# A tenth gate and up pair by seven products in place of two whole hidden tiles, in a two-layer encoder

## The chip, the cores and the metric

The kernel runs on one core of one Trainium2 chip. Its time is the device time of one launch in microseconds (us); the median over the runs is compared. Engines are named as in the profile: PE (TensorE, with PEld for its weight loads), DVE (VectorE), ACT (ScalarE), POOL (GpSimd) and SP (SyncE, which here issues DMAs).

## The reference, cut to what matters

Two encoder layers over 512 tokens of width 1024, in float32. Each has an attention part and a feed-forward part (SwiGLU), each part with a root-mean-square norm in front of it and one behind it:

```
for layer in range(2):
    h = rms_norm(x, attn_pre_g[layer])
    y = mla_mixer(h, ...) if layer == 0 else chunked_mixer(h, ...)
    x = x + rms_norm(y, attn_post_g[layer])
    h = rms_norm(x, ffn_pre_g[layer])
    f = (silu(h @ w_gate) * (h @ w_up)) @ w_down      # 1024 -> 2816 -> 1024
    x = x + rms_norm(f, ffn_post_g[layer])
```

The change concerns `h @ w_gate` and `h @ w_up` of both layers and the steps just ahead of them.

## The kernel before, in words

Activations are kept transposed: features on the 128 partitions, 512 tokens along the row. x is eight tiles of 128 x 512. A matrix product is done in three passes on numbers split into a high and a low part (`split`, lines 143 to 149: ScalarE makes the high part, VectorE the low part as the difference); `mm3` (line 376) is the three matmuls high x high, high x low and low x high. So each weight chunk that is loaded (a `raw` tile, 128 x 1024, of which there are five) costs a cast on ScalarE, `whi`, and a subtraction on VectorE, `wlo`, before TensorE can use it. There are three buffers of split weights.

`Feed` (line 264) holds the plan of all weight chunks in the order of their use. `feed.next` hands out the next chunk and first calls for the split of the chunks behind it, one or two ahead; `feed.ahead` calls for more of them early. `feed.behind[n]` names instructions that the split of chunk n has to be queued behind on their engines; `behind` and `tc.issue_after` do the same for other instructions. Otherwise each engine's order of work follows the order in which the program writes its instructions: the earlier written goes first, but one that isn't ready lets later ones pass, as planned when the program is built. `first(n)` puts an instruction n places forward. On the chip each engine works its list in that order.

**The feed-forward part, `ffn` (line 1134).** The attention's output projection (`out_proj`, line 687) runs its last two groups in two halves of 256 tokens each. Behind each half the post norm's squares are summed (`Post.half`, `Post.add_half`, line 634), and `Post.apply` (line 667) adds the normed result to x half by half and splits x into `xs` (lines 672, 674, 148 and 149). x itself is fetched from memory at the start of `ffn` (`fetch`, line 679).

The hidden width 2816 is 22 tiles of 128, and each needs a gate and an up product over K = 1024. Before the change:

- Tiles f = 0 and 1 (weights `w_gu0`) are made in two halves of 256 tokens, `half(0)` and `half(1)`, as x becomes ready.
- Tiles f = 2 and 3 (weights `w_gu`) are made whole, 512 tokens a matmul, by `proj` (line 382): 96 matmuls.
- The other 18 tiles are nine pairs (`products`, line 1520). A pair takes its two gate and two up tiles by the seven products of Strassen's scheme instead of eight: rows of K and tokens are halved, sums of weight blocks are multiplied with sums of x blocks. Each product j = 0 to 6 is 24 matmuls of 256 columns, 168 in a pair. The x-sums `tb` are made once a layer by `blocks_of` (line 1315) in three steps, `next(more)` each: the first gives what product 0 uses, the second product 3, the third products 4 and 5; products 1, 2 and 6 use x itself. The weight sums are made by accumulating DMAs on the GpSimd queue (`Pair.begin`, line 164, called for the next pair during this one) and by VectorE (`Pair.sums`, line 182); for the first pair, VectorE makes all of them.

The results of a pair are gathered in `gate` and `up_` tiles as its products end (lines 1553 to 1566). After product 6 come the gates: times the norm's factor `rb` (line 1567), silu on ScalarE (1568), times up (1570), and `Hidden.add` (line 1257), which makes four sums of 256 columns out of two tiles. The norm of the feed-forward's input is applied there, on the outputs. Its squares (`sx.squares`, line 760) are summed over the partitions by four transposes (`tot`, line 473), raised to the power -1/2 on GpSimd (483) and spread by four transposes (`bc`, 501) while the whole tiles run.

In the second layer `by_tokens` (line 1215) also transposes the kept x on VectorE during the pairs. `down` (line 1286) multiplies by `w_down`, again by seven products.

PSUM has eight banks: four called `mm`, two `s` and two `t`. Hidden tiles and x-sums' intermediates lie in a pool `h` of 40 tiles, x, its splits and the splits of the x-sums in a pool `u` of 39.

Of the kernel before, what the change touches and what calls it, by code (L numbers as in the profile page):

```python
# [14 lines left out]
OP = mybir.AluOpType  # L15
# [12 lines left out]
N_WHOLE = 4  # L28
# [40 lines left out]
def trunk(ctx: ExitStack, tc: tile.TileContext, a, out):  # L69
# [80 lines left out]

    class Pair:
# [4 lines left out]
        def __init__(self, src):  # L156
            self.src, self.raw, self.then, self.made = src, {}, None, False

        def tile(self, n, pool_=wp, tag="raw", bufs=5):
            t = pool_.tile([P, 1024], F32, tag=tag, name=name_("raw"), bufs=bufs)  # L160
            nc.sync.dma_start(t, self.src[n])
            return t

        def begin(self):

            r, self.made = self.raw, True
# [6 lines left out]
        def load(self, j):  # L173

            if j == 0:
                if not self.made:
                    self.raw[4] = self.tile(2, wide[0], "sum2", 2)
                self.raw[5] = self.tile(3)
            elif j in (1, 2):
                self.raw[j] = self.tile(j - 1)  # L180

        def sums(self, j):
# [4 lines left out]
            if j == 0 and not self.made:  # L187
                r[0] = r[3] = r[6] = wide[0].tile([P, 1024], F32, tag="sum", name=name_("raw"), bufs=2)
                plus(r[0], r[4], r[5])
            elif j in (3, 6):  # L190
                plus(r[j], r[j], r[j // 3])
            elif j == 4 and not self.made:
                plus(r[4], r[4], r[1])
            elif j == 1 and self.then:
                self.then.begin()
# [68 lines left out]
    class Feed:  # L264


        def __init__(self):
            self.plan, self.raw, self.ready, self.pos, self.room = [], [], [], 0, {}
            self.behind, self.gate, self.low = {}, None, None
# [4 lines left out]
        def add_pairs(self, src):  # L274
# [14 lines left out]
        def load(self, i):  # L289
            while len(self.raw) <= min(i, len(self.plan) - 1):  # L290
# [5 lines left out]
                if isinstance(src, Pair):  # L296
                    src.load(j)
# [314 lines left out]
    class Post:  # L612
# [21 lines left out]
        def add_half(self, h, banks, rest, n1, n2, end=None):  # L634
# [32 lines left out]
        def apply(self, x, h, each, to=None):  # L667
            c = HALF[h]
            for k in range(KT):
                t = self.y[k][:, c]  # L670
                with first(80 * h):
# [5 lines left out]
                    each(k, h)  # L677

    def fetch(src, make=U):
        x = []  # L680
        for k in range(KT):
            t = make(name="x")
            nc.sync.dma_start(t, src[:, k])
            x.append(t)
        return x

    def out_proj(rhs, n_k, post, have, n_last, late):
# [35 lines left out]
        for h in range(2):  # L723
# [17 lines left out]
            if not h:  # L741
                feed.ahead(3)
# [40 lines left out]
    def plan_ffn(i):  # L783
        for c in range(4):
            feed.add(a["w_gu0"][i, c], 1024, room="h")
        for f in range(N_WHOLE - 2):
            for c in range(2):
                feed.add(a["w_gu"][i, f, c], 1024)
# [345 lines left out]
    def ffn(i, x_src, osp, firsts, late=()):  # L1134
# [38 lines left out]
        tb = []  # L1173
        more = blocks_of(x, G_FPRE[i], H, tb)
        next(more)
        b = [bank(), bank()]
        rest = proj(2, KT, 4, xs, b)
        some(rest, 3)
        v = sx.sum.total()
        r = rstd(v)  # L1180
        eps = sp.tile([P, 4], F32, tag="eps", name=f"eps_{i}", bufs=1)
        V.tensor_scalar(eps, v, EPS, None, op0=OP.mult)
        some(rest, 7)
        rb = spread_sb(r)
        next(more)
        banks.extend(b)
        hid = Hidden(H)


        for f in range(N_WHOLE):  # L1190
            if f < 3:
                b = banks[2 * f:2 * f + 2]
                if f == 2:
                    run(rest)
            else:
                b = [bank(), bank()]
                run(proj(2, KT, 4, xs, b))
            t = U(name="gt")
            V.tensor_tensor(t, b[0], rb, op=OP.mult)
            nc.scalar.activation(t, t, AF.Silu)  # L1200
            h = hid.room()
            V.scalar_tensor_tensor(h, t, -1.0, b[1], op0=OP.mult, op1=OP.mult)
            hid.add(h)
            if f == 1:
                next(more)
        products(xs, tb, rb, hid, by_tokens(H) if i else None)
# [108 lines left out]
    def blocks_of(x, gain, make, out):  # L1315
# [3 lines left out]
        for k in range(KT // 2):  # L1319
            out.append([(U(F32R, "th"), U(F32R, "tl")) for _ in range(2)])  # L1320
# [9 lines left out]
        for k in K2:  # L1330
# [3 lines left out]
            split(*cut(out[k][0], A1), m[:, A1])  # L1334
        yield
        for k in K2:
# [3 lines left out]
            split(*out[k][1], n)  # L1340
        yield

    class After:
# [3 lines left out]
        def __init__(self, layer, eps, make):  # L1347
# [4 lines left out]
            self.x, self.later = None, []  # L1352
# [74 lines left out]
        def during(self, j, i):  # L1427
            if j == Down.E3 and i == 1:
                self.x = fetch(a["mid"])
# [90 lines left out]
    def products(xs, tb, rb, hid, aside=None):  # L1520
# [5 lines left out]
                  [cut(xs[k + K2], A1) for k in range(K2)]]  # L1526
        pairs = (NF - N_WHOLE) // 2
        for p in range(pairs):
            al, ga = [], []
            be = [bank("t" if p % 2 else "s", "be") for _ in range(2)]  # L1530
            gate = [U(name="gt") for _ in range(2)]
            up_ = [U(name="ut") for _ in range(2)]
            for j in range(7):
# [10 lines left out]
                for e in range(2):  # L1544
# [10 lines left out]
                    elif j == 1:  # L1555
                        nc.scalar.copy(t[:, A0], o)
                    elif j == 2:
                        V.tensor_tensor(t[:, A0], t[:, A0], o, op=OP.add)
# [6 lines left out]
                    else:  # L1565
                        V.tensor_tensor(t[:, A1], t[:, A1], o, op=OP.add)
                        V.tensor_tensor(t, t, rb, op=OP.mult)
                        nc.scalar.activation(t, t, AF.Silu)
                        h = hid.room()
                        V.tensor_tensor(h, t, u, op=OP.mult)  # L1570
                        hid.add(h)
# [286 lines left out]
```

## Time and profile before

| | us |
|---|---|
| median of 3 runs | 1105.76 (1105.74 to 1106.14) |
| profiled execution | 1109.37 |
| its span, first to last instruction | 1107.4 |

The columns of the page's engine table are busy time, share of the span and count. Rows of the timeline give the start, the length, engine, line, operation, result<-inputs and shape, and in brackets the idle time before it with what ended it; a length includes an end that overlaps the next instruction, so that the distance between starts is the price in a full queue. Rows of the waits give the time waited in all, how often and the longest.

### The profile page before, as it was taken

Reading aid. Unit: us, or ns where it says so; the run is one execution under the profiler, and the core shown is the slowest. Engines: PE = TensorE matmul, PEld = TensorE weight load, DVE = VectorE, ACT = ScalarE, POOL = GpSimd, SP = SyncE. Lnnn points to the kernel's source line nnn. Section 1 sums busy time; section 2 is a strip of 40 time slices with the busy share of each in tenths; the row PEclk is TensorE's granted clock in tenths of the full one; section 3 lists DMA queues with packets and bytes.
Section 4 is the critical chain, followed back from the end, with each engine's and each line's share of the span. In section 5 each row is a group of like instructions: output and inputs, shape, how many; then the busy total and the mean of one; then the engine's idle time right before and its main releaser. Section 6 shows DMA issues by size and latency. Waiting matters only on the chain. (4 is left out here: it accounts for less than half of the span.)

```text
span 1107.4 us, 19059 instructions
## 1 busy us (share of the span) xinstructions
PE 1094.4 (99%) x6893; PEld 979.9 (88%) x6893; DVE 909.3 (82%) x1659; ACT 680.5 (61%) x1323; POOL 117.1 (11%) x181
## 2 busy tenths in 40 slices
PE   9999999999999999999999999999999999999997
PEld 6887889999999998888888888889999999998885
DVE  6787747988878879978857898758988889789977
ACT  7476638555555556668636677657645555556675
POOL 1211100100000001500000110000100010001401
PEclk9999999999999999999999999999999999999999
DMA  7444216538778657961556677634638878858913
GB/s 238 114 122 125 79 59 227 161 103 194 173 196 202 161 184 236 162 192 49 190 152 154 179 192 186 160 128 162 186 106 214 227 197 212 233 176 247 173 29 76
DMA packets 88335, 181.47 MB, mean 164 GB/s; under 512 B 26817, under 2 KB 28609, under 8 KB 88241
## 3 DMA queue, kind: packets, MB, share of 16 engines
q1 hardware_dynamic: 74752, 147.10, 43.5%
q0 software_dynamic: 13056, 32.73, 16.8%
q8 instruction: 54, 0.88, 0.3%
q10 hardware_dynamic: 432, 0.44, 0.1%
q14 instruction: 41, 0.33, 0.1%
HBM read 148.88 MB, written 10.88 MB: 144 GB/s over the span
## 5 line engine op out<-in xcount | busy, mean ns | idle before, releaser
L144 ACT CAST whi<-raw 128x1024 fp32r<-128x1024 f32 (+3 forms) x220 | 221.7, 1008 | 208.7 <-PE al L1550 69.4
L145 DVE TENSOR_TENSOR wlo<-raw,whi 128x1024 fp32r<-128x1024 f32 (+3 forms) x220 | 256.5, 1167 | 69.4 <-ACT whi L144 68.3
L1550 PE MATMUL al<-th,whi 128*128 128x256 f32 x432 | 122.9, 284 | 0.2 <-ACT gt L1560 0.2
L1550 PE MATMUL al<-tl,whi 128*128 128x256 f32 x432 | 121.1, 280 | 0.0
L1550 PE MATMUL al<-th,wlo 128*128 128x256 f32 x432 | 121.1, 280 | 0.0
L377 PE MATMUL b<-xh,whi 128*128 128x512 f32 x234 | 96.7, 414 | 0.0
L379 PE MATMUL b<-xh,wlo 128*128 128x512 f32 x234 | 91.9, 393 | 0.2 <-DVE wlo L145 0.2
L378 PE MATMUL b<-xl,whi 128*128 128x512 f32 x234 | 91.7, 392 | 0.0
L1550 PEld LDWEIGHTS al<-th,whi 128*128 128x128 f32 x432 | 81.4, 188 | 2.5 <-ACT gt L1560 0.4
L1550 PEld LDWEIGHTS al<-tl,whi 128*128 128x128 f32 x432 | 81.4, 189 | 0.0
L1550 PEld LDWEIGHTS al<-th,wlo 128*128 128x128 f32 x432 | 81.4, 188 | 0.0
L548 ACT ACTIVATE p<-p,mn 128x128 f32<-128x128 f32 (+1 forms) x96 | 54.3, 565 | 35.2 <-DVE mn L546 33.3
L145 DVE TENSOR_TENSOR ptl<-pt,pth 128x128 fp32r<-128x128 f32 (+1 forms) x96 | 46.7, 487 | 31.1 <-ACT pth L144 30.2
L145 DVE TENSOR_TENSOR wlo<-wd,whi 128x512 fp32r<-128x512 f32 x86 | 56.5, 689 | 14.6 <-ACT whi L144 14.4
L144 ACT CAST whi<-wd 128x512 fp32r<-128x512 f32 x86 | 49.9, 619 | 25.0 <-PE al L1306 10.7
L144 ACT CAST pth<-pt 128x128 fp32r<-128x128 f32 (+1 forms) x96 | 40.5, 424 | 32.1 <-PE pt L561 31.2
L171 POOL DMA_DIRECT2D raw<-in_w_pair x32 | 28.1, 897 | 287.9 <-DMA raw<-in_w_pair 94.6
L379 PEld LDWEIGHTS b<-xh,wlo 128*128 128x128 f32 x234 | 43.9, 188 | 10.5 <-DVE wlo L145 0.9
L1306 PE MATMUL al<-whi,pl 128*128 128x512 f32 x132 | 51.5, 390 | 0.0
L1306 PE MATMUL al<-whi,ph 128*128 128x512 f32 x132 | 51.4, 390 | 0.0
L1306 PE MATMUL al<-wlo,ph 128*128 128x512 f32 x132 | 51.3, 389 | 0.0
L184 DVE TENSOR_TENSOR raw<-raw,raw 128x1024 f32<-128x1024 f32 x40 | 48.9, 1223 | 0.5
(320 smaller groups left out, 3393.7 us busy)
## 6 DMA issues: line engine op xcount, KB each, us to landing
raw<-in_w_pair SPq DMA_DIRECT2D x88, 512.0 KB, 4.6
raw<-in_w_pair POOLq DMA_DIRECT2D x32, 512.0 KB, 7.5
wd<-in_w_down SPq DMA_DIRECT2D x54, 256.0 KB, 5.7
raw<-in_w_o SPq DMA_DIRECT2D x16, 512.0 KB, 3.8
raw<-in_w_gu SPq DMA_DIRECT2D x16, 512.0 KB, 4.8
raw<-in_w_down SPq DMA_DIRECT2D x16, 512.0 KB, 4.4
raw<-in_w_qkb SPq DMA_DIRECT2D x16, 512.0 KB, 3.6
wd<-in_w_down POOLq DMA_DIRECT2D x22, 256.0 KB, 5.4
```

What stands on the lines that cost most here:

```text
L144: return (nc.scalar.copy(dst_hi, src), V.tensor_tensor(dst_lo, src, dst_hi.bitcast(F32), op=OP.subtract))
L145: V.tensor_tensor(dst_lo, src, dst_hi.bitcast(F32), op=OP.subtract))
L171: nc.gpsimd.dma_start(r[j], self.src[n], accum_op=OP.add)
L184: V.tensor_tensor(t, x, y, op=OP.add)
L377: nc.tensor.matmul(o, l[0], r[0], start=start, stop=False)
L378: nc.tensor.matmul(o, l[0], r[1], start=False, stop=False)
L379: last_mm[0] = nc.tensor.matmul(o, l[1], r[0], start=False, stop=stop)
L548: nc.scalar.activation(p[:, :n], p[:, :n], AF.Exp, bias=mn[:, :1], scale=-1.0, accum_out=self.sums[:, qt:qt + 1])
L1306: nc.tensor.matmul(to[e], l[c], r[d], start=j < 4 and k == 0 and n == 0, stop=k == NF // 2 - 1 and n == 2, skip_group_check=True)
L1550: nc.tensor.matmul(o, l[c], r[d], start=first_ and n == 0, stop=k == K2 - 1 and n == 2, skip_group_check=True)
```

## The change

The two whole tiles go and a tenth pair takes their place: only tiles 0 and 1 stay as they are (`N_WHOLE` is 2). The first pair follows `half(1)` directly. Its weight sums are begun like the others' by DMAs, and it takes its products in the order 1, 2, 0, 3, 6, 4, 5. The first two steps of `blocks_of` are written ahead of the first pair, the third at its product 0. The four banks of tiles 0 and 1 are copied to `kept` tiles by ScalarE.

The squares of x are taken in the second pair, the norm's sum and spread in the third, and with them the gates of tiles 0 and 1. The gates of pairs one to three are held back: they are written at (2,6), (3,1) and (3,4), where (p, j) is product j of pair p counted from 0. From the fourth pair on the gates come at the end of the pair as before. x is fetched behind the loads of the first pair's first weights, and the splits of the next six weights are queued behind the post norm's last squares as well as behind its factor.

```diff
-N_WHOLE = 4
+N_WHOLE = 2
...
+    FIRST_TURN = (1, 2, 0, 3, 6, 4, 5)
...
+            if not h:
+                with behind(feed.loaded):
+                    next(p for p, *_ in feed.plan[feed.pos:] if isinstance(p, Pair)).begin()
             for n in range(len(feed.ready), len(feed.ready) + 6):
-                feed.behind[n] = fence
+                feed.behind[n] = fence + ins
...
             if not h:
-                feed.ahead(3)
+                feed.ahead(3 if late else 5)
+                feed.loaded = get_x(feed.loads[feed.pos + 5])
...
-        x = fetch(x_src)
+        x = []
         post = Post(G_APOST[i], H)
-        last = out_proj(osp, KT, post, firsts, 2, late)
+        last = out_proj(osp, KT, post, firsts, 2, late, lambda after: fetch(x_src, x, after))
...
-        sx.squares(0)
-        post.apply(x, 1, sx.each)
+        feed.behind[next(n for n in range(feed.pos, feed.pos + 9) if feed.plan[n][2] == 0)] = post.apply(x, 1, sx.each)
+        tb, hid = [], Hidden(H)
+        more = blocks_of(x, G_FPRE[i], H, tb)
+        next(more)
         run(half(1))
-        sx.squares(1)
...
+        kept = [H(name="fu") for _ in banks]
+        for t, b in zip(kept[:2], banks[:2]):
+            nc.scalar.copy(t, b)
+        turned = next(more)
+        feed.behind[feed.pos + 3] = turned
+        with behind(turned[0]):
+            for t, b in zip(kept[2:], banks[2:]):
+                empty = nc.scalar.copy(t, b)
...
+        def gates():
+            for f in range(N_WHOLE):
+                t, u = kept[2 * f:2 * f + 2]
+                V.tensor_tensor(t, t, rb[0], op=OP.mult)
+                nc.scalar.activation(t, t, AF.Silu)
+                h = hid.room()
+                V.scalar_tensor_tensor(h, t, -1.0, u, op0=OP.mult, op1=OP.mult)
+                hid.add(h)
...
+        def step():
+            feed.behind[feed.pos + 3] = next(more)
+
+        side = {(0, 0): step, (1, 1): lambda: sx.squares(0), (1, 4): lambda: sx.squares(1), (2, 1): norm,
+                (2, 3): spread_, (2, 4): gates, (2, 6): lambda: held[0](), (3, 1): lambda: held[1](),
+                (3, 4): lambda: held[2]()}
+        products(xs, tb, rb, hid, side, held, (empty, turned[1]), by_tokens(H) if i else None)
...
-            for j in range(7):
+            for j in (range(7) if p else FIRST_TURN):
+                if (p, j) in side:
+                    side[p, j]()
                 if aside is not None and p and j in (0, 1, 3, 5):
                     next(aside, None)
                 w = feed.next(1024, 2)
...
+                        if p > 2:
+                            gated(t, u)
+
+            if p < 3:
+                held.append(lambda gate=gate, up_=up_: [gated(t, u) for t, u in zip(gate, up_)])
```

`norm` is the sum of the squares and the power, `spread_` the four transposes `bc` with their copy, `gated` the gate steps of a pair as before. The rest of the diff lays out the weights for ten pairs, hands the new arguments through, and takes the held gate and up tiles of the first three pairs from pool `h`.

More of the change, by code (lines that the diff above doesn't have):

```diff
@@ L149, in split_scaled @@
                 V.scalar_tensor_tensor(dst_lo, src, col, dst_hi.bitcast(F32), op0=OP.mult, op1=OP.subtract))
+    FIRST_TURN = (1, 2, 0, 3, 6, 4, 5)
     class Pair:
         def __init__(self, src):
-            self.src, self.raw, self.then, self.made = src, {}, None, False
+            self.src, self.raw, self.then, self.turn = src, {}, None, range(7)
         def tile(self, n, pool_=wp, tag="raw", bufs=5):
             t = pool_.tile([P, 1024], F32, tag=tag, name=name_("raw"), bufs=bufs)
-            nc.sync.dma_start(t, self.src[n])
+            self.last = nc.sync.dma_start(t, self.src[n])
             return t
         def begin(self):
-            r, self.made = self.raw, True
+            r = self.raw
             r[0] = r[3] = r[6] = self.tile(2, wide[0], "sum", 2)
@@ L186, in sums @@
             r = self.raw
[L187 to L190, printed above, removed]
+            if j in (3, 6):
                 plus(r[j], r[j], r[j // 3])
-            elif j == 4 and not self.made:
-                plus(r[4], r[4], r[1])
-            elif j == 1 and self.then:
+            if j == (3 if self.turn[0] else 1) and self.then:
                 self.then.begin()
@@ L268, in __init__ @@
             self.plan, self.raw, self.ready, self.pos, self.room = [], [], [], 0, {}
-            self.behind, self.gate, self.low = {}, None, None
+            self.behind, self.gate, self.low, self.loads = {}, None, None, {}
         def add(self, src, n, gain=None, room=None):
@@ L279, in add_pairs @@
                 pair.then = pairs[p + 1] if p + 1 < n else None
-                for j in range(7):
+                if not p:
+                    pair.turn = FIRST_TURN
+                for j in pair.turn:
                     self.plan.append((pair, 1024, j, None))
@@ L296, in load @@
                 if isinstance(src, Pair):
-                    src.load(j)
+                    self.loads[len(self.raw)] = src.load(j)
                     self.raw.append(None)
@@ L676, in apply, with fetch, out_proj @@
                         (nc.gpsimd if k in (0, 2, 4) else V).tensor_tensor(to(k), x[k][:, c], t, op=self.op)
[L677 to L687, printed above, removed]
+                    at = each(k, h)
+            return at
+    def fetch(src, x, after=None):
+        with behind(after):
+            for k in range(KT):
+                t = U(name="x")
+                ins = nc.sync.dma_start(t, src[:, k])
+                x.append(t)
+        return ins
+    def out_proj(rhs, n_k, post, have, n_last, late, get_x):
         done = list(have)
@@ L1176, in ffn @@
[L1176 to L1180, printed above, removed]
-        eps = sp.tile([P, 4], F32, tag="eps", name=f"eps_{i}", bufs=1)
[L1182 to L1205, printed above, removed]
@@ L1206, in ffn, with norm @@
-        products(xs, tb, rb, hid, by_tokens(H) if i else None)
+        kept = [H(name="fu") for _ in banks]
[6 more added lines that the diff above has]
+                empty = nc.scalar.copy(t, b)
+        eps = sp.tile([P, 4], F32, tag="eps", name=f"eps_{i}", bufs=1)
+        rb = []
+        def norm():
+            v = sx.sum.total(None, 300)
+            with first(300):
+                r = rstd(v)
+            V.tensor_scalar(eps, v, EPS, None, op0=OP.mult)
+            rb.append(r)
@@ L1319, in blocks_of @@
         for k in range(KT // 2):
-            out.append([(U(F32R, "th"), U(F32R, "tl")) for _ in range(2)])
+            out.append([tuple(m(F32R, n) for n in ("th", "tl")) for m in (U, make if k == 3 else U)])
         K2 = range(KT // 2)
@@ L1518, in plus_x, with products @@
                 queue.dma_start(rows_of(i)[:, o * S:o * S + S][:, c], t[:, c])
-    def products(xs, tb, rb, hid, aside=None):
+    def products(xs, tb, rb, hid, side, held, turned, aside=None):
         K2 = KT // 2
```

48 lines of the change are left out of this document (23 added, 25 removed).

## The prediction

> **What bounds the kernel now.** I read the page first: its engine table, then who waited for whom on TensorE, then the busy time of the engines in the stretches that the change replaces.
>
> ```profile
> span 1107.4 us, 19059 instructions
> PE 1094.4 (99%) x6893; PEld 979.9 (88%) x6893; DVE 909.3 (82%) x1659; ACT 680.5 (61%) x1323; POOL 117.1 (11%) x181
> ```
>
> ```profile
> PE bc L501 <- POOL r L483: 0.9, 2, 0.7
> PE b L377 <- ACT y L621: 0.8, 1, 0.8
> PE al L1550 <- ACT gt L1560: 0.2, 1, 0.2
> ```
>
> ```profile
> core 0: us, PE busy (x) PEld busy (x) DVE busy (x) ACT busy (x) POOL busy (x), PEclk, DMA share, GB/s
> 213.64:236.39 22.75, 22.75 (x106) 18.81 (x105) 20.36 (x42) 13.70 (x23) 2.91 (x3) 1.00 0.33 70
> 236.39:256.30 19.91, 19.91 (x169) 19.77 (x168) 17.16 (x25) 10.98 (x17) 0.87 (x1) 1.00 0.58 154
> 256.30:276.20 19.90, 19.90 (x170) 19.77 (x169) 16.68 (x24) 10.95 (x17) 2.16 (x3) 1.00 0.76 185
> 790.60:813.32 22.72, 22.72 (x107) 18.80 (x105) 20.63 (x44) 13.84 (x23) 3.22 (x3) 1.00 0.33 71
> 813.32:833.03 19.71, 19.71 (x169) 19.71 (x168) 16.89 (x24) 10.98 (x17) 0.84 (x1) 1.00 0.54 154
> ```
>
> TensorE is busy for 99% of the span, and the waits of its instructions in the feed-forward layers are the three rows above, under 2 us together. So it is the bound there: whatever takes matmul time away shortens the run, as long as nothing new makes TensorE wait. The third view shows where such a wait could come from. Its first and fourth rows are the two whole hidden tiles that the change replaces (f = 2 and 3 of layers 1 and 2); the rows behind them are pairs. VectorE is busy for 20.4 of 22.8 us in the whole tiles and 16.7 of 19.9 in a settled pair. It has 2 to 3 us to spare in each, and no more.
>
> **TensorE's work.** Two whole tiles are 96 matmuls of 512 columns, a pair is 168 of 256. The whole tiles' stretch also holds eight small transposes, for the norm's sum and its spread, which the change keeps and moves into the third pair:
>
> ```profile
> 215.72 0.60 PE L473 MATMUL tot<-ident,acc 128*128 128x128 f32 x4
> 216.07 0.48 PE L377 MATMUL b<-xh,whi 128*128 128x512 f32 x1
> 220.96 0.60 PE L501 MATMUL bc<-ident,r 128*128 128x128 f32 x4
> 221.32 0.48 PE L377 MATMUL b<-xh,whi 128*128 128x512 f32 x1
> ```
>
> From start to start they take 0.35 + 0.36 = 0.71 us. So a layer gives up 22.75 - 0.71 = 22.04 us and gets 19.90 for the tenth pair: 2.1 us less, and 4.2 us less in both layers (22.72 in the second). An eighth of the arithmetic would be 2.8 us in a layer; the rest goes because a column costs more in narrow matmuls, 22.04 / 96 = 0.230 us for 512 against 19.90 / 168 = 0.118 for 256. [...] The trace has durations for both, and I stay with 4.2.
>
> **VectorE's queue in the first pair.** The 22 us that go were also cover: behind them VectorE made the x-sums (`blocks_of`) and the squares, before a pair needed anything. Now the first pair starts when the first two tiles end (213.64 in this trace), and its product j = 6, the fifth in its turn, is due 4 x 2.84 = 11.4 us later, at 225.0. Durations from start to start:
>
> ```profile
> 199.81 0.75 DVE L672 TENSOR_TENSOR y<-y,bc 128x256 f32<-128x256 f32 x2
> 200.47 0.76 DVE L674 TENSOR_TENSOR x<-x,y 128x256 f32<-128x256 f32 x2
> ...
> 201.47 0.89 DVE L149 SCALAR_TENSOR_TENSOR xl<-x,gains,xh 128x256 fp32r<-128x256 f32 x2
> 202.28 0.42 DVE L674 TENSOR_TENSOR x<-x,y 128x256 f32<-128x256 f32 x1
> ```
>
> ```profile
> 276.76 0.42 DVE L1566 TENSOR_TENSOR gt<-gt,be 128x256 f32<-128x256 f32 x1
> 277.21 0.69 DVE L1567 TENSOR_TENSOR gt<-gt,bc 128x512 f32<-128x512 f32 x1
> 277.82 1.22 DVE L145 TENSOR_TENSOR wlo<-raw,whi 128x1024 fp32r<-128x1024 f32 x1
> 278.96 1.29 DVE L1570 TENSOR_TENSOR hd<-gt,ut 128x512 f32<-128x512 f32 x2
> 280.16 0.42 DVE L1271 TENSOR_TENSOR hs<-hd 128x256 f32<-128x256 f32 x1
> 280.50 0.42 DVE L1273 TENSOR_TENSOR hs<-hd,hd 128x256 f32<-128x256 f32 x1
> 280.83 0.42 DVE L1272 SCALAR_TENSOR_TENSOR hs<-hs,hd 128x256 f32<-128x256 f32 x1
> 281.17 1.22 DVE L145 TENSOR_TENSOR wlo<-raw,whi 128x1024 fp32r<-128x1024 f32 x1
> 282.30 0.42 DVE L1274 SCALAR_TENSOR_TENSOR hs<-hs,hd 128x256 f32<-128x256 f32 x1
> 282.64 1.22 DVE L184 TENSOR_TENSOR raw<-raw,raw 128x1024 f32<-128x1024 f32 x1
> 283.77 1.22 DVE L145 TENSOR_TENSOR wlo<-raw,whi 128x1024 fp32r<-128x1024 f32 x1
> ```
>
> So 256 columns take 0.34 us, an `xl` 0.40, 512 columns 0.60, a weight's low half (`wlo`) or weight sum 1.14. VectorE can begin the second half of `apply` at 199.81, as now. What the program puts ahead of product 6's weights is then: `apply`, 8 x (0.34 + 0.34 + 0.40) = 8.6; the x-sums of the first two steps, 16 x 0.34 = 5.4, and of the third, 8 x 0.34 + 4 x 0.60 = 5.1; the weights of j = 0 and 3, one of them a sum first, 3 x 1.14 = 3.4; the two additions of j = 2, 0.7; and its own sum and low half, 2.3. That is 25.5 us from 199.81, so 225.3: 0.3 us late if VectorE never pauses. The third step is written ahead of product 6's weights though only j = 4, behind it, needs it. Bounds: nothing if the order slips in favour of product 6, 2.5 if the ScalarE cast between the sum and the low half (1 us) is not covered and the weights of j = 4 go first (1.1). I take 1.2 us in each layer, the middle. That `begin` now leaves the first pair's two weight sums to DMAs costs VectorE nothing and saves it 2.3, counted above. The four bank copies and the first two steps' casts lie on ScalarE, busy for 13.7 of 22.75 us here: nothing.
>
> **VectorE's queue in the third and fourth pairs.** A pair's own list is seven low halves (8.0), two sums (2.3) and six additions (2.0), 12.2 us. Its gates are 2 x 0.61 + 2 x 0.60 + 4 x 0.34 = 3.8 more, together 16 of 19.9. The change holds the gates of the whole tiles and of pairs one to three until the norm's spread, ahead of product j = 3 in the third pair, and issues them at (2,4), (2,6), (3,1) and (3,4). Pairs three and four have 2 x (19.9 - 12.2) = 15.4 us for them, of which the first four sevenths of pair three, 4.4 us, have gone by; four lots of 3.8 us are 15.0. In the queue: three lots stand ahead of the weights of product j = 3 of pair four. From about 1 us before (2,4) to the start of (3,3) are 6 x 2.84 + 1 = 18.0 us; in it belong 11.3 of gates, the low halves of j = 6 and of four more products and one sum, 6.8, and four additions, 1.3: 19.4, so 1.4 late. VectorE can't run far ahead, since a weight's cast waits until TensorE has done with the buffer, three products back:
>
> ```profile
> ACT whi L144 <- PE al L1550: 69.4, 63, 1.7
> ```
>
> That lead is used up in this count. Bounds: nothing, if the lead is a product larger, and 3.4 if the sum of j = 6 and one low half more are still to be made. I take 1.6 in each layer. In the second layer transposes of the kept x fall into the same stretch:
>
> ```profile
> L1222 DVE STREAM_TRANSPOSE xt<-x x8: 703/709/715, 841.8 to 942.9; 128x512 f32<-128x512 f32 x8
> ```
>
> One or two of 0.7 us: 0.6 more there, between 0 and 1.4. Squares fall into pair two, where no gates stand now: 16 x 0.34 = 5.4 against 7.7 free, nothing.
>
> **x fetched later, splits behind the post norm.** The eight x tiles are now issued behind the loads of the first pair's weights:
>
> ```profile
> L683 SPq DMA_DIRECT2D x<-in_x x8: 328/439/710, 164.0 to 168.6; - x8
> ...
> DMA to landing us min/median/max: 5.8/6.3/7.4
> ```
>
> ```profile
> 169.90 9.63 SPq L303 DMA_DIRECT2D raw<-in_w_gu x6
> ```
>
> ```profile
> 185.64 0.42 DVE L674 TENSOR_TENSOR x<-x,y 128x256 f32<-128x256 f32 x1
> ```
>
> The six weight loads behind x now go out until 179.5; four of them will go ahead of it. So by my estimate x is issued from about 176 to 181 and lands, 6.3 us later, from 182 to 187. The first tile is wanted at 185.64 and each next about 1.1 us later. I take nothing; 2 us a layer if the weight buffers free up late. On the other side, weight casts are now put behind the post norm's squares, and this is a wait of layer 2 that can go:
>
> ```profile
> 757.49 1.05 ACT L144 CAST whi<-raw 128x1024 fp32r<-128x1024 f32 x1 [0.46 <-DMA raw<-in_w_gu]
> 758.45 0.65 ACT L457 ACTIVATE sq<-b 128x256 f32<-128x256 f32 x2
> ```
>
> ScalarE casts a weight while the squares wait, and TensorE then stands 0.8 us for `y` and 0.7 for `r` (the waits at the top). I take 1.0 of it as won; between 0 and 1.7. The queues of SyncE and GpSimd carry two more accumulating loads a layer for the first pair, issued 20 us before they are needed, at a DMA share of 0.33: nothing.
>
> **The sum.** -4.2 + 2 x (1.2 + 1.6) + 0.6 - 1.0 = +1.0 us. The profiled execution took 1109.37 us (span 1107.4 and 2.0 around it), 3.6 above the runs' median of 1105.76; applied to that median, 1106.8. About 0.2%, 2.2 us, is what a measurement of this kernel can tell from no change, so this is no change.
>
> **The rivals.** *VectorE's lateness costs more than TensorE gains, and it is slower.* Same places, upper prices: the gates' queue at product j = 3 of the fourth pair at 2.6 and again at the next sums, the first pair at 1.9: -4.2 + 2 x 4.5 + 0.6 - 0.5 = +4.9, 1110.7. It decides once a layer loses over 3.2 us. For it: VectorE's free 3.2 us in a pair, and an order in which gates precede weights. Against: nothing waits for the gates themselves, so a different order in the queue frees TensorE. *The lead absorbs the lots, and it is faster.* If the order puts weights first, 0.5 in each layer stays: -4.2 + 1.0 + 0.3 - 1.0 = -3.9, 1101.9. For it: TensorE waits 0.2 us in all of the present pairs; and VectorE idles in pair two and the front of pair three, so the overload is short. Against: the two counts above, which exceed their time without any pause. *x comes late:* +2 to +4, 1109 to 1111, if buffers hold the loads in front of it; by that estimate its first tile has 3 us to spare. *The norm's gates don't move as written,* because the order of instructions is computed from priorities: that would be the faster case.
>
> **How the numbers follow.** No change 0.36, the faster case 0.28, the gates' queue at its upper price 0.32, x late 0.04. So faster by over 0.2% 0.28, within 0.36, slower 0.36. The forecast's own range is 1103.6 to 1108.0. Going out to the two rivals' times, 1101.6 to 1110.8 leaves out the ends at which several bounds hold together, some 2 in 10.
>
> **What would show it.** Right: stretches of a whole tile gone and ten pairs of 19.9 us; TensorE idle before `al` of product j = 3 of the fourth pair with VectorE's `wlo` as releaser, 1 to 3 us; a like wait at `be` of j = 6 in the first pair; the waits for `y` and `r` near 759 us gone. Wrong: no `wlo` among TensorE's waits (then about 1101.9), a wait for an `xh` or `xl` while the first two tiles run, or pairs that take other than 19.9 us once they have settled.

## The result, and the profile after

| | us |
|---|---|
| before, median of 4 runs beside it | 1105.95 (1105.74 to 1106.81) |
| after, median of 4 runs | 1122.11 (1120.42 to 1122.86) |
| ratio | 1.0139, 95% interval 1.0126 to 1.0152 |
| profiled execution after, and its span | 1122.81, 1121.0 |

The kernel became 1.4% slower, 16 us, and the time lies 11 us above the end of the predicted range. The page of the kernel after, against a span of 1107.4 us and 1094.4 us of TensorE before:

```profile
span 1121.0 us, 19399 instructions
...
PE 1095.9 (98%) x7037; PEld 987.4 (88%) x7037; DVE 919.3 (82%) x1677; ACT 692.3 (62%) x1353; POOL 124.9 (11%) x189
...
PEclk9999999989999999999999999999999999999999
```

TensorE's busy time did not fall, though it has less arithmetic. One digit points to the reason: in the ninth slice the granted clock is an 8, where before all digits were 9. Next the waits of TensorE's instructions (what waited, for whom, us in all, times, the longest):

```profile
PE be L1566 <- ACT whi L144: 5.7, 2, 2.9
PE al L1566 <- DVE ut L1580: 3.1, 3, 1.7
PE be L1566 <- DVE wlo L145: 2.7, 3, 1.2
...
PE al L1566 <- DVE wlo L145: 0.5, 1, 0.5
```

The seven products (line 1566 now) waited 0.2 us in all before, and now 12. The wait of `b` for `y` in layer 2's output projection is gone. The stretches of the first five pairs (in layer 2, of pairs one, three and four) tell where the time went:

```profile
core 0: us, PE busy (x) PEld busy (x) DVE busy (x) ACT busy (x) POOL busy (x), PEclk, DMA share, GB/s
213.80:239.65 25.85, 23.00 (x171) 22.51 (x170) 20.36 (x35) 15.59 (x29) 1.73 (x2) 0.87 0.47 133
239.65:259.88 20.23, 19.98 (x171) 19.77 (x170) 17.09 (x28) 14.58 (x32) 0.86 (x1) 1.00 0.57 168
259.88:282.23 22.35, 21.10 (x179) 20.85 (x178) 18.96 (x33) 13.79 (x21) 4.02 (x4) 1.00 0.61 166
282.23:303.62 21.39, 20.27 (x171) 19.91 (x170) 21.10 (x34) 12.01 (x20) 1.45 (x2) 1.00 0.65 170
303.62:323.66 20.04, 20.04 (x171) 19.92 (x170) 17.36 (x25) 10.86 (x17) 2.13 (x3) 1.00 0.71 183
...
796.50:821.57 25.07, 21.93 (x171) 21.26 (x169) 20.34 (x35) 15.59 (x29) 1.71 (x2) 0.93 0.47 141
...
841.95:864.36 22.41, 21.17 (x179) 20.91 (x178) 19.74 (x33) 13.70 (x21) 3.61 (x3) 1.00 0.93 238
864.36:886.95 22.59, 20.38 (x171) 19.96 (x170) 22.31 (x36) 12.08 (x20) 1.72 (x2) 1.00 0.71 173
```

A settled pair takes 19.9 to 20.0 us, as predicted. The first pair takes 25.9 and 25.1, the third 22.4 (0.7 of it the moved transposes), the fourth 21.4 and 22.6. The account of the two traces, in us (a settled pair is 19.91):

| where | change |
|---|---|
| two whole tiles (22.04) for one settled pair (19.91), two layers | -4.2 |
| first pairs over 19.91 | +5.9 and +5.2 |
| second pairs over 19.91 | +0.3 and +0.5 |
| third pairs over 19.91 and 0.71 of transposes | +1.7 and +1.8 |
| fourth pairs over 19.91 | +1.5 and +2.7 |
| later pairs, against the excess of the nine pairs before | -0.8 |
| layer 2 from layer 1's last pair to the first two tiles' end (373.1 against 397.4 less the whole tiles' 22.7) | -1.6 |
| the rest (ahead of layer 1's pairs, behind layer 2's) | +0.7 |
| sum, against 13.6 of the spans | +13.7 |

The two spans lie 13.6 us apart and the medians 16.2, because the profiled execution of the kernel before was itself 3.6 us above its median.

The first pair is the largest item, and it holds two things. Here it is by stretch (same columns):

```profile
222.00:225.00 3.00, 3.00 (x28) 3.00 (x26) 3.00 (x8) 1.45 (x3) 0.00 (x0) 1.00 0.00 0
225.00:228.00 3.00, 0.22 (x2) 0.02 (x1) 2.54 (x4) 2.19 (x5) 0.00 (x0) 0.92 0.07 10
...
229.00:232.00 3.00, 3.00 (x14) 2.71 (x13) 2.63 (x3) 1.18 (x2) 0.00 (x0) 0.50 0.75 268
232.00:234.00 2.00, 2.00 (x12) 2.00 (x11) 0.42 (x1) 0.04 (x1) 0.80 (x1) 0.50 0.94 279
234.00:235.00 1.00, 1.00 (x9) 1.00 (x9) 0.42 (x1) 1.00 (x1) 0.07 (x1) 0.82 0.92 328
235.00:236.00 1.00, 1.00 (x10) 1.00 (x10) 0.96 (x1) 0.01 (x1) 0.21 (x1) 1.00 1.06 229
```

From 225 to 228 TensorE does next to nothing (0.22 us): product 6, the fifth in turn, waits 2.85 us for its weights. Then the granted clock (the third number from the end) is 0.50 for 6.83 us, from 227.53 to 234.36: from 229 to 232, 14 matmuls are done in 3 us, where 28 were done from 222 on. In layer 2 it is 0.50 to 0.69 from 811 to 815. And this is why the weights are late, in VectorE's timeline:

```profile
214.95 0.43 DVE L1339 SCALAR_TENSOR_TENSOR t<-t,xg 128x256 f32<-128x256 f32 x1 [0.68 <-ACT xg L1338]
...
218.64 0.42 DVE L1344 TENSOR_TENSOR t<-xg,xg 128x256 f32<-128x256 f32 x1
...
225.12 0.68 DVE L145 TENSOR_TENSOR tl<-t,th 128x512 fp32r<-128x512 f32 x1
225.72 1.22 DVE L185 TENSOR_TENSOR raw<-raw,raw 128x1024 f32<-128x1024 f32 x1
226.86 0.68 DVE L145 TENSOR_TENSOR tl<-t,th 128x512 fp32r<-128x512 f32 x1
228.05 3.58 DVE L145 TENSOR_TENSOR wlo<-raw,whi 128x1024 fp32r<-128x1024 f32 x3 [0.51 <-ACT whi L144]
```

The third step of the x-sums (lines 1344, 1345 and their `tl`) runs from 218.64 and product 6's weight sum (line 185) only at 225.72, when product 6 is already due; the cast and the low half follow. VectorE also came to this point late: from 199.25 on it had paused eight times for ScalarE (the first row is the longest of these pauses), 3.2 us in all until 228.05.

### The profile page after: what moved, and what is told of

The parts are those of the page before. It is cut to its first block, busy times and chain, and to the rows that moved or that the text cites. A ratio compares the mean times of both kernels' runs of the same rounds, so it can differ in the third digit from the quotient of the medians.

```text
span 1121.0 us, 19399 instructions
## 1 busy us (share of the span) xinstructions
PE 1095.9 (98%) x7037; PEld 987.4 (88%) x7037; DVE 919.3 (82%) x1677; ACT 692.3 (62%) x1353; POOL 124.9 (11%) x189
## 4 chain that ended last, share of the span: by engine, by line
PE 86%; DVE 8%; ACT 2%; DMA 2%; issue 1%; POOL 0%; SPq 0%; DVEq 0%; POOLq 0%; ACTq 0%
PE al L1566 15%; PE b L375 10%; PE b L376 10%; PE b L377 10%; PE be L1566 9%; PE al L1312 8%; PE be L1312 5%; PE ga L1566 4%; PE de L1312 3%; PE ga L1312 3%; DVE wlo L145 2%; PE pt L559 2%; PE b L1725 2%; PE b L1107 1%; DMA x<-in_x 1%
## 5 line engine op out<-in xcount | busy, mean ns | idle before, releaser
L144 ACT CAST whi<-raw 128x1024 fp32r<-128x1024 f32 (+4 forms) x226 | 226.9, 1006 | 191.8 <-PE al L1566 68.1
L145 DVE TENSOR_TENSOR wlo<-raw,whi 128x1024 fp32r<-128x1024 f32 (+4 forms) x226 | 262.7, 1165 | 67.8 <-ACT whi L144 66.5
L1566 PE MATMUL al<-th,whi 128*128 128x256 f32 x480 | 137.2, 286 | 3.3 <-DVE ut L1580 3.1
L1566 PE MATMUL al<-th,wlo 128*128 128x256 f32 x480 | 134.4, 281 | 0.5 <-DVE wlo L145 0.5
L1566 PE MATMUL al<-tl,whi 128*128 128x256 f32 x480 | 134.5, 280 | 0.0
L1566 PEld LDWEIGHTS al<-th,whi 128*128 128x128 f32 x480 | 90.6, 189 | 6.4 <-DVE ut L1580 3.7
L375 PE MATMUL b<-xh,whi 128*128 128x512 f32 x170 | 71.8, 422 | 0.0
L377 PE MATMUL b<-xh,wlo 128*128 128x512 f32 x170 | 67.1, 395 | 0.3 <-DVE wlo L145 0.3
L376 PE MATMUL b<-xl,whi 128*128 128x512 f32 x170 | 66.8, 393 | 0.0
L1566 PE MATMUL be<-xh,whi 128*128 128x256 f32 x160 | 46.6, 293 | 5.7 <-ACT whi L144 5.7
```

The lines of the kernel that those rows point to most:

```text
L144: return (nc.scalar.copy(dst_hi, src), V.tensor_tensor(dst_lo, src, dst_hi.bitcast(F32), op=OP.subtract))
L145: V.tensor_tensor(dst_lo, src, dst_hi.bitcast(F32), op=OP.subtract))
L375: nc.tensor.matmul(o, l[0], r[0], start=start, stop=False)
L376: nc.tensor.matmul(o, l[0], r[1], start=False, stop=False)
L377: last_mm[0] = nc.tensor.matmul(o, l[1], r[0], start=False, stop=stop)
L1566: nc.tensor.matmul(o, l[c], r[d], start=first_ and n == 0, stop=k == K2 - 1 and n == 2, skip_group_check=True)
```

## The experiments

My theory: VectorE's written order makes TensorE wait 3 us in each first pair; that idle halves the clock for some microseconds behind it (3 us more); and the lots of held gates cost 3 to 4 us in pairs three and four. Rivals: the half clock comes from the load there (the DMA share rises to 0.75 to 1.06 in the same microseconds, and products 6 and 4 are mixed); VectorE has too much to do, in any order; the waits behind have a cause other than the gates. The ratios are to the kernel before, run beside each kernel on the same chip. The medians come from different chips, so the ratios are what can be compared.

| kernel | median us | ratio, 95% interval | first pair, us (layers 1, 2) |
|---|---|---|---|
| after | 1122.11 | 1.0139 (1.0126 to 1.0152) | 25.85, 25.07 |
| 1 third step later | 1118.21 | 1.0107 (1.0089 to 1.0125) | 24.39, 24.35 |
| 2 gates later | 1122.34 | 1.0137 (1.0116 to 1.0158) | 25.85, 25.46 |
| 3 both of these | 1117.43 | 1.0100 (1.0082 to 1.0117) | 22.86, 24.34 |
| 4 filler | 1118.69 | 1.0105 (1.0086 to 1.0125) | 23.85, 23.90 |
| 5 before, norm's line alone | 1103.64 | 0.9981 (0.9972 to 0.9990) | none changed |
| 6 third step in halves | 1113.56 | 1.0067 (1.0053 to 1.0081) | 21.53, 21.53 |
| 7 gates in half lots | 1119.03 | 1.0118 (1.0104 to 1.0132) | 24.97, 25.49 |
| 8 both of 6 and 7 | 1109.89 | 1.0033 (1.0021 to 1.0046) | 21.53, 21.53 |
| 9 as 8, work on GpSimd | 1116.38 | 1.0088 (1.0071 to 1.0104) | 21.91, 21.90 |
| 10 as 9, squares on GpSimd | 1116.79 | 1.0093 (1.0078 to 1.0107) | 21.94, 21.91 |

**1: the third step later.**

```diff
-            feed.behind[feed.pos + 3] = next(more)
+            feed.behind[feed.pos + 2] = next(more)
-        side = {(0, 0): step, (1, 1): lambda: sx.squares(0), (1, 4): lambda: sx.squares(1), (2, 1): norm,
+        side = {(0, 3): step, (1, 1): lambda: sx.squares(0), (1, 4): lambda: sx.squares(1), (2, 1): norm,
```

> The kernel after, with the third step of the x-sums written behind the weight sum and low half of product 6 in the first pair (at product 3 in place of product 0). Queue theory: TensorE's wait ahead of product 6 falls from 3.0 us to under 1 us in each layer and the granted clock stays at 1.00 there, so 5 to 6 us less per layer: 1110 to 1112 us. Load theory (the half clock comes from the DMA load and the mixed order of products in that stretch): the clock still falls to 0.5 for 4 to 6 us, so at most the 3 us of waiting per layer go: 1116 us or more.

It took 4 us off, not ten. The wait ahead of product 6 nearly went, from 2.85 us, as expected, but product 4, the next, now waits twice, first for the cast of its weights and then for their low half:

```profile
229.65 0.39 PE L1566 MATMUL al<-th,whi 128*128 128x256 f32 x1 [1.51 <-ACT whi L144]
...
231.05 0.38 PE L1566 MATMUL al<-th,wlo 128*128 128x256 f32 x1 [0.67 <-DVE wlo L145]
```

```profile
229.00:231.00 2.00, 0.73 (x4) 0.53 (x4) 2.00 (x4) 2.00 (x3) 0.87 (x1) 1.00 0.25 23
...
232.00:235.00 3.00, 3.00 (x16) 3.00 (x16) 1.60 (x3) 0.08 (x1) 0.00 (x0) 0.50 1.02 242
```

And the clock fell to 0.50 behind it again. My expectation had taken the wait for one that goes; it moved. By its number this run fits the load theory; experiments 3 and 4 decide between the two.

**2: the gates later.** In this kernel and the next the hidden tiles of pairs three and four enter the down projection in exchanged places. So their output is not that of the reference; the amount of work is the same.

```diff
-                (2, 3): spread_, (2, 4): gates, (2, 6): lambda: held[0](), (3, 1): lambda: held[1](),
-                (3, 4): lambda: held[2]()}
+                (2, 3): spread_, (2, 4): gates, (3, 0): lambda: held[0](), (3, 5): lambda: held[1](),
+                (4, 3): lambda: held[2]()}
```

> The kernel after, with the held gates of pairs one to three written at (3,0), (3,5) and (4,3) in place of (2,6), (3,1) and (3,4). Queue theory: the waits in pairs three and four, 3 to 4 us in each layer, mostly go and the half clock in the first pair stays: 2 to 3.5 us less per layer, 1115 to 1118 us. Rival, the late weight sums come by DMA and not from the gates: within 1.5 us of 1122.

No gain in the median: the expectation was missed. The stretches of layer 1's fourth pair and layer 2's fifth show both halves of the reason:

```profile
280.44:300.47 20.03, 20.03 (x171) 19.85 (x169) 19.53 (x29) 11.80 (x20) 1.75 (x2) 1.00 0.71 184
...
881.71:903.76 22.05, 20.14 (x171) 19.93 (x170) 19.86 (x32) 10.92 (x17) 0.85 (x1) 1.00 0.74 212
```

```profile
890.32 0.71 DVE L1228 STREAM_TRANSPOSE xt<-x 128x512 f32<-128x512 f32 x1 [1.65 <-DMA x<-mid]
```

The fourth pair is well (20.03 in place of 21.39, in layer 2 20.14 in place of 22.59), so the gates' place was the cause there. But pair three keeps its 22.3, and in layer 2 the loss went on to pair five, 22.05 in place of 20.00: VectorE stands 1.65 us before a transpose of the kept x whose load has not landed, with weights and additions queued behind.

**3: both.**

```diff
-            feed.behind[feed.pos + 3] = next(more)
+            feed.behind[feed.pos + 2] = next(more)
...
+        side = {(0, 3): step, (1, 1): lambda: sx.squares(0), (1, 4): lambda: sx.squares(1), (2, 1): norm,
+                (2, 3): spread_, (2, 4): gates, (3, 0): lambda: held[0](), (3, 5): lambda: held[1](),
+                (4, 3): lambda: held[2]()}
```

> Both edits together: the third step of the x-sums later, and the held gates later. Queue theory: the two savings add up, 1101 to 1106 us, at or a little below the kernel before. Load theory: 1112 us or more, with the clock still at 0.5 for some us in the first pair of each layer.

The time lies 11 us above what my theory gave and, as in experiment 1, within what the load theory gave, but this kernel tells more than its time. In both layers the first pair waits as in the first experiment. In layer 1 the clock stays, in layer 2 it falls. The first two rows are of layer 1, the others of layer 2; each time the first holds the long wait:

```profile
229.00:231.00 2.00, 0.73 (x4) 0.54 (x4) 2.00 (x4) 2.00 (x4) 0.87 (x1) 1.00 0.00 0
...
232.00:235.00 3.00, 3.00 (x27) 3.00 (x26) 2.87 (x5) 0.99 (x1) 0.00 (x0) 1.00 0.98 210
...
807.00:809.00 2.00, 0.47 (x5) 0.36 (x4) 2.00 (x5) 1.97 (x3) 0.37 (x1) 1.00 0.44 167
...
811.00:814.00 3.00, 3.00 (x17) 3.00 (x16) 1.74 (x4) 0.36 (x1) 0.00 (x0) 0.52 0.96 233
```

At a DMA share of 0.98 the clock is 1.00 in layer 1 and at 0.96 it is 0.52 in layer 2. So the load does not set it. It also isolates the price: 22.86 against 24.34 us for the same work and the same waits (1.51 and 0.67 us, 1.53 and 0.67), 1.5 us for the half clock alone.

**4: work in place of the idle time.**

```diff
+        def filler():
+            w = bank("t", "fill")
+            for _ in range(13):
+                nc.tensor.matmul(w, xs[0][0][:, :P], xs[0][0], start=True, stop=True)
...
+        side = {(0, 0): step, (0, 6): filler, (1, 1): lambda: sx.squares(0), (1, 4): lambda: sx.squares(1), (2, 1): norm,
```

> The kernel after, with 13 more matmuls of 512 columns (3.0 us) written ahead of product 6 of the first pair of each layer, on operands that are long ready; their result is not used. TensorE then works in the time in which it waited. Idle time sets the clock: the granted clock stays at 1.00 behind it, and the 2 to 3 us of slow matmuls in each layer go though the work is more: 1115 to 1118 us. Load theory: the clock falls to 0.5 as before, and the time is 1121 us or more.

```profile
225.29 3.12 PE L1212 MATMUL fill<-xh 128*128 128x512 f32 x13
```

```profile
228.00:230.00 2.00, 1.55 (x10) 1.04 (x9) 1.70 (x2) 2.00 (x4) 0.00 (x0) 1.00 0.82 252
230.00:235.00 5.00, 4.99 (x44) 4.82 (x42) 4.36 (x7) 1.60 (x3) 0.87 (x1) 1.00 0.82 269
```

The clock stays at 1.00 in both layers, under the same DMA share and the same mixing of products, and useless work makes the kernel 3 to 4 us shorter (the expectation ended at 1118, 0.7 us lower). With the wait of 2.9 us filled and the load still there (a DMA share of 0.82 from 230 to 235 and of 0.95 from 810 to 815), the half clock goes. So in these first pairs the cause is TensorE's idle time: 0.50 behind 2.85 us of it in the kernel after, 1.00 here. The load theory falls.

**5: one line of the change on the kernel before.**

```diff
-                feed.behind[n] = fence
+                feed.behind[n] = fence + ins
```

> The kernel before, with only one line of the change: the splits of the next six weights are queued behind the post norm's squares as well as behind its factor. Theory: this line is what took the wait for y in layer 2's output projection away (0.84 us, and about 1.75 us in that stretch of the two traces); no more than 1.8 us less than the kernel before, 0.5 at least. Rival, the gain there came from the later fetch of x or the earlier weights: no difference over 0.3 us, and the wait for y is still in the trace.

```profile
PE sc L1094 <- ACT kh L144: 1.9, 1, 1.9
PE warm L113 <- DVE idle L110: 1.2, 1, 1.2
PE bc L501 <- POOL r L483: 0.7, 1, 0.7
```

These three rows are the whole view of its waits; that for `y` is gone, that for `r` is not. The stretch in layer 2 between the pairs of layer 1 and the first two tiles' end is 1.7 us shorter than before, the same as in the kernel after (1.6). So this line alone made that gain, and it beats both kernels: 0.19%, some 2.1 us, under the kernel before, with an interval that leaves 1 out (at most 1.8 us was expected, which lies within that interval).

**6: the third step in halves, each behind the weights that are due ahead of it.**

```diff
             V.tensor_tensor(n[:, A0], v[:, A1], u[:, A1], op=OP.subtract)
+            last = split(*cut(out[k][1], A0), n[:, A0])
+        yield last
+        for k in K2:
+            u, v, m, n = ts[k]
             V.scalar_tensor_tensor(n[:, A1], m[:, A1], -1.0, v[:, A0], op0=OP.mult, op1=OP.subtract)
-            last = split(*out[k][1], n)
+            last = split(*cut(out[k][1], A1), n[:, A1])
...
+        side = {(0, 3): step, (0, 6): step, (1, 1): lambda: sx.squares(0), (1, 4): lambda: sx.squares(1), (2, 1): norm,
```

> As the first experiment (third step later), but the third step is also cut in two: the 256 columns that product 4 uses are made first, and those that product 5 uses behind product 4's weights. No work is left out. Order theory: each part of VectorE's list has its own due time, and with the parts in the order of use the first pair loses under 1 us per layer and keeps its clock, 20 to 21 us instead of 24.4: 1109 to 1112 us. Amount theory: VectorE has too much to do there in any order, and the wait moves once more, behind product 4: first pair 22.5 us or more, 1115 us or more.

```profile
213.62:235.15 21.53, 20.57 (x171) 19.99 (x170) 18.84 (x38) 16.11 (x33) 1.73 (x2) 1.00 0.48 126
...
791.71:813.24 21.53, 20.50 (x170) 19.93 (x169) 18.84 (x38) 16.10 (x33) 1.71 (x2) 1.00 0.49 136
```

With the same work in the order of use the first pair takes 21.53 us in both layers in place of 25.85 and 25.07, and the clock stays at 1.00; the time falls by 0.7%, some 8 us. The time lies between the two expectations: order was most of it. 1.6 us are left, 0.8 to 1.0 of them ahead of product 5, whose bank waits for an addition of product 4, behind VectorE's list. VectorE is busy without a pause from 225 to 236 us, so from there on the rest is amount. But before that it pauses for ScalarE: in 8, whose first pair takes the same 21.53 us, 0.82 us ahead of 217.53 and 0.47 ahead of 218.76. Whether the rest comes from the amount of VectorE's work or from these hand-overs was not tried apart.

**7: the gates in half lots.**

```diff
-                (2, 3): spread_, (2, 4): gates, (2, 6): lambda: held[0](), (3, 1): lambda: held[1](),
-                (3, 4): lambda: held[2]()}
+                (2, 3): spread_, (2, 4): lambda: gates(0), (2, 6): lambda: gates(1)}
+        for n in range(10):
+            at = 22 + 2 * n
+            side[at // 7, at % 7] = lambda n=n: held[n]()
...
-            if p < 3:
-                held.append(lambda gate=gate, up_=up_: [gated(t, u) for t, u in zip(gate, up_)])
+            if p < 5:
+                held.extend(lambda t=t, u=u: gated(t, u) for t, u in zip(gate, up_))
```

> The kernel after, with the held gates handed out in half lots (one hidden tile at a time), one at every second product from (2,4) to (5,5), for which the gates of pairs four and five are held too. Theory of lumps: VectorE has 1.1 us free in each product and a half lot is 1.9, so one in two products fits; the waits of pairs three and four (3.1 us in layer 1 and 4.3 in layer 2) fall to under 1 us a layer, 1115 to 1118 us, with the first pair unchanged. Rival, the late sums and low halves there have another cause (the squares, the norm, DMAs): 1120 us or more.

Pairs three and four take 21.12 and 20.12 us in layer 1 and 21.13 and 20.05 in layer 2, so 2.5 and 3.8 us less together, with the same gates: the lumps were the cause there. But the time gains only 0.2%, 1 us short of the expectation, as layer 2's fifth pair takes 22.08, 2.2 over a settled pair (outside the first pairs TensorE's longest wait in this trace is 1.7 us, for an addition to `ut`).

**8: both.** Its edits are those of experiments 6 and 7.

> Both of these edits together. If the change's loss is only VectorE's list in the first pair, the clock behind it, and the lumps of gates, then the tenth pair's 4.2 us and the 1.7 us of layer 2's output projection stay: 1102 to 1106 us, below the kernel before on the same chip by 0.1 to 0.4%. If something else costs too, it is 1108 us or more.

1.06% below the kernel after, and still 0.3% above the kernel before: the theory's expectation was missed, something else costs too. Its ten pairs take 202.6 and 205.0 us, where ten of 19.91 and the transposes would be 199.8. So 2.8 and 5.2 us of waits are left, 8.0 in all, more than the 4.2 and 1.6 us that the change wins. The largest are the 1.6 us of each first pair and 1.7 in layer 2's pair five (21.61 us), where VectorE stands before a load again:

```profile
877.98 0.71 DVE L1230 STREAM_TRANSPOSE xt<-x 128x512 f32<-128x512 f32 x1 [1.74 <-DMA x<-mid]
```

**9: the third step's subtractions on GpSimd, the transposes later.** These two edits stand beside those of 8.

```diff
-            V.tensor_tensor(n[:, A0], v[:, A1], u[:, A1], op=OP.subtract)
+            nc.gpsimd.tensor_tensor(n[:, A0], v[:, A1], u[:, A1], op=OP.subtract)
...
-                if aside is not None and p and j in (0, 1, 3, 5):
+                if aside is not None and p > 3 and j in (0, 1, 3, 5):
```

> The version of the last experiment (third step in halves, gates in half lots) with the four subtractions that begin the third step on GpSimd in place of VectorE, and layer 2's transposes of x from the fifth pair on. GpSimd is idle there (its 64 x 512 operations take 1.29 us, so some 0.65 us for 256 columns, beside VectorE's 0.34). Theory: the first pair's last wait is VectorE's amount of work, so with 1.4 us less of it the 1.0 us wait ahead of product 5 goes in both layers, and in layer 2 the 1.7 us of pair five, where VectorE stands before a transpose for its DMA: 3 to 4 us less, 1105 to 1107 us. Rival, GpSimd takes the place as the late one (its work is slower or holds VectorE up): first pair as before or longer, 1109 us or more.

The rival came true. GpSimd's row, and VectorE's in the same microseconds:

```profile
214.18 3.63 POOL L1346 TENSOR_TENSOR t<-xg,xg 128x256 f32<-128x256 f32 x4 [14.33 <-ACT xg L1340]
```

```profile
215.37 0.96 DVE L145 TENSOR_TENSOR tl<-t,th 128x256 fp32r<-128x256 f32 x1
216.25 0.96 DVE L1341 SCALAR_TENSOR_TENSOR t<-t,xg 128x256 f32<-128x256 f32 x1
217.13 0.96 DVE L145 TENSOR_TENSOR tl<-t,th 128x256 fp32r<-128x256 f32 x1
218.02 0.42 DVE L1341 SCALAR_TENSOR_TENSOR t<-t,xg 128x256 f32<-128x256 f32 x1
```

While GpSimd subtracts, at 0.9 us each, VectorE's operations go from 0.34 to 0.88 us from start to start; the next, behind its end, has 0.42 again. So the offload cost VectorE what it should have saved. The transposes' edit did what it should in the pairs (205.0 to 202.9 us in layer 2), but behind them more was lost: layer 2's end, from its last pair on, takes 120.8 us in place of 114.2. The down projection waits, and the clock falls there too (0.60):

```profile
1000.09 0.51 PE L1314 MATMUL al<-whi,ph 128*128 128x512 f32 x1 [2.00 <-ACT ph L144]
1001.92 0.79 PE L1314 MATMUL al<-whi,pl 128*128 128x512 f32 x1 [0.86 <-DVE pl L145]
```

```profile
1002.00:1006.00 4.00, 3.76 (x9) 2.64 (x9) 2.26 (x4) 0.16 (x1) 0.00 (x0) 0.60 0.47 71
```

Two of the moved transposes lie in VectorE's list there, at 991.96 and 1001.77; that they are the cause was not tried apart from the other edit.

**10: the squares' additions on GpSimd too.** This edit stands beside those of 9.

```diff
-                    ins += V.tensor_tensor(t, t, q[:, c], op=OP.add),
+                    ins += self.engine.tensor_tensor(t, t, q[:, c], op=OP.add),
...
         def squares(self, h):
+            self.sum.engine = nc.gpsimd
```

> The same, and the additions of the squares in the second pair (14 of 256 columns in each layer, 4.8 us of VectorE) on GpSimd too. Theory: the second and third pairs lose their last 0.4 and 0.5 us in each layer: 1 to 2 us less than the version without it, 1103 to 1106 us, below the kernel before and about where the one line of the norm alone lies. Rival: no gain, since those waits come from the additions of product 4 in the order of the queue, or a loss, if GpSimd's sums are late for the norm's transposes in the third pair.

The second pair loses its last 0.3 us in each layer (19.93 and 19.76 us), the third pair none, and the median is no better than that of 9, so this expectation was missed too. GpSimd spends 15.7 us on twelve of the additions.

## Why the prediction was wrong, point by point

The step that failed is the price of the first pair, 1.2 us a layer. It cost 5.9 and 5.2 us: the wait was mis-sized, ScalarE's part in it was put at nothing, and what follows a wait had no term at all. The gates' queue was mis-sized too. The prediction's own upper bounds for both queues and the transposes together, with nothing won at the post norm, give 1114.8 us, still 7 us short.

- **TensorE's work, -4.2:** right. Settled pairs are 19.91 to 20.04 us.
- **VectorE's queue in the first pair, 1.2 a layer, at most 2.5:** the step that failed. Place and mechanism were right (product 6 waits, for the third step is written ahead of its weights), the size was not: 3.0 and 3.6 us of waits, counted from start to start (the rows have 2.85, and 2.90 with 0.23 behind it). I had counted the list as done without a pause. Between 199.25 and 228.05 VectorE paused for 3.2 us, in steps of 0.15 to 0.68, each time for ScalarE: steps of the x-sums pass between both engines, and "VectorE never pauses" was not what the trace of before could promise.
- **ScalarE in the first pair, 0:** wrong, and a part of the same step. I had taken its busy share over the whole stretch (13.7 of 22.75 us) as room. In the trace of after, the chain of work that ended last runs almost wholly through ScalarE from 212.92 to 220.76, and ScalarE is busy for 7.64 of these 7.84 us: the four bank copies (0.59 us each by their rows) stand in its list among the products with the gains (line 1338) and the casts for which VectorE waits. In experiment 9 TensorE itself waits 0.6 us for such a copy. No run moves the copies, so what they cost alone stays open.
- **What an idle TensorE costs behind the wait:** missing altogether. Each price in the sum was that of the wait itself. Of the first pairs' 5.9 and 5.2 us over, 3.0 and 3.6 are waits; the half clock added about the other 2.9 and 1.6. The trace of before had a sign of it that the page's digits do not show: behind a wait of 1.92 us in the attention part (line 1094) its clock is 0.50 from 109.46 to 112.87. In the kernel after, a wait of 2.85 us was followed by 0.50 for 6.83 us (layer 1) and one of 2.90 by 0.50 for 3.41 us (layer 2); the last section has what the traces show of shorter ones.
- **The gates' queue, 1.6 a layer, at most 3.4:** the mechanism was right, the size was 3.2 and 4.5 in pairs three and four. The predicted wait (`al` of product 3 in pair four, for `wlo`) is there in layer 2, 0.5 us; larger are two that I had not named: `be` of product 6 in pair three, right behind the first lot (1.2 in both layers), and product 5 in pair four, whose bank is free only after an addition to `ut` that stands behind gates (up to 1.7). I had looked at the weights alone; an addition that empties a bank is as much a debt in VectorE's queue. Experiments 2 and 7 show that the lots are the cause in pair four, experiment 7 in pair three too.
- **Layer 2's transposes, 0.6:** in that stretch 1.3 more than in layer 1; whether it is their 0.7 us each was not tried for the kernel after. In other placements of the gates they cost more, through their loads (1.65 us in experiment 2, 1.74 in 8).
- **The post norm's wait in layer 2, -1.0, at most -1.7:** right for `y`, 1.6 to 1.7 in size (experiment 5). The wait for `r`, which was to go with it, is still there, 0.7 us in both kernels.
- **x fetched later, the DMA queues: 0.** Right: x was issued from 178 to 182 us, the first tiles' stretch has no wait for x, and the account's rest is 0.7 us.
- **The rivals:** the slower case was named, with its decision point at over 3.2 us lost in a layer. A layer lost 9 to 10 us, so the direction of that rival came true, with less than half of its cost in its sum (4.5 us a layer).

## What to carry to other kernels

Before work is taken out of a stretch, ask what it covered: here 22 us of TensorE hid a chain between VectorE and ScalarE whose length is not the sum of its busy time but includes their hand-overs. Place side work by the due time of what stands behind it in the queue, in pieces not larger than the slack of one step, and count additions that free banks as well as weights. Where TensorE may stand for 2 to 3 us, price the clock behind it too (here 0.50 for 3.41 to 6.83 us), and shorten such a wait or fill it; two waits close together can count as one (here 1.5 and 0.7 us, 0.7 us apart).

## What the runs showed of the hardware

- **Idle time and the clock.** A single wait of some 2.9 us was followed by a granted clock of 0.50 to 0.53 in all six first pairs that had one (after, 2 and 7). Two waits of 1.5 and 0.7 us, 0.7 us apart, were followed by 0.50 in layer 1 of 1 and 0.52 in layer 2 of 3, and by 1.00 in layer 1 of 3. Single waits of up to 1.71 us in after, and 1.91 us of idle time in layer 2's fifth pair of 2, left the clock at 1.00. In 9, 2.0 and 0.9 us in the down projection were followed by 0.60 from 1002 to 1006. The wait at line 1094, 1.92 us in before and 1.93 in after, was followed by 0.50 in both.
- **How long, and what goes ahead.** In the traces of before and after, away from the ends of the launch, three stretches of 0.50 last 3.41 us and one 6.83. In after, 116.05 and 576.85 us lie between them, 34 and 169 times 3.413. Cut into pieces of that length, in line with these stretches, the two traces have, away from the ends, four pieces at full clock that a stretch of 0.50 follows, with TensorE idle for 1.75 us (before, from 106.04), 1.93, 2.31 and 2.90 us (after, from 104.65, 224.12 and 807.80). A piece with 1.70 us idle (after, from 879.48) was followed by 1.00, as was each with 1.25 us or less. That the place of a wait on such a grid decided between the two layers of 3 is an estimate from these numbers, not shown there. In the kernel before, the wait at line 1094 lay almost wholly in one piece (1.67 of 3.42 us busy) and the next ran at 0.50:

```profile
106.04:109.46 3.42, 1.67 (x10) 1.46 (x11) 3.15 (x5) 2.68 (x6) 1.04 (x3) 1.00 0.62 151
109.46:112.87 3.41, 3.41 (x14) 3.31 (x14) 3.13 (x9) 1.73 (x5) 0.35 (x1) 0.50 0.84 311
```

- **GpSimd and VectorE.** In 9, four subtractions of 256 columns took 3.63 us on GpSimd, 0.9 each, and VectorE's operations beside them took 0.88 us from start to start, against 0.34 without. By what means the one holds the other, no run shows.
- **A load can stop VectorE.** A transpose whose input had not landed held VectorE's queue for 1.65 us in 2 and 1.74 in 8; TensorE stands for 1.91 and 1.14 us in these pairs (22.05 less 20.14, 21.61 less 20.47).
